# Turning the decayed keys of a gated-linear-attention loop by DMA instead of TensorE

## The chip, the cores and the metric

The kernel is one program on one core of one Trainium2 chip. The metric is the device time of one execution in microseconds (us): the median of several runs. The engines are named as the profile names them: PE is TensorE (matrix products), PEld its loading of the stationary operand, DVE is VectorE, ACT ScalarE, POOL GpSimd, and SP the sequencer that issues nearly all DMA transfers of this kernel. Each engine runs its own list of instructions strictly in the order fixed when the program was built; an instruction whose operand is not ready holds up all that stand behind it on its engine.

## The reference

One denoising step of a network of width 1024 with two layers, on 256 context tokens and 1024 latent tokens, 1280 tokens in all. Layer 0 mixes tokens by gated linear attention (GLA) in both directions, layer 1 by softmax attention. Each layer ends in a gate and an output projection. The part that the change touches is the recurrence of layer 0, of which there is one for each of 4 heads and 2 directions:

```python
def step(S, inp):
    qi, ki, vi, gi = inp
    b = jnp.cumsum(gi, axis=2)
    b_last = b[:, :, -1:, :]
    qe = qi * jnp.exp(b)
    ke = ki * jnp.exp(-b)
    a = jnp.where(mask, jnp.einsum("bhtk,bhsk->bhts", qe, ke), 0.0)
    o = jnp.einsum("bhts,bhsv->bhtv", a, vi) + jnp.einsum("bhtk,bhkv->bhtv", qe, S)
    S = jnp.exp(b_last[:, :, 0, :])[..., None] * S + jnp.einsum(
        "bhsk,bhsv->bhkv", ki * jnp.exp(b_last - b), vi)
    return S, o
```

Here `g` is the logarithm of a decay that depends on the token (`log_sigmoid(h @ wa1 @ wa2 + ba) / 16`), `ke` are the decayed keys, `a` is the masked score matrix of a chunk and `S` the state (128 keys by 256 values a head). The results are the two token streams, the GLA states after the context, and the attention layer's context keys and values, all in float32.

## The kernel before, in words

**Stages.** After a short prologue (modulation, normalised tokens turned into `hT_hi` and `hT_lo`, two f16 halves that together stand for float32), a long loop does the GLA layer, from about 80 to 520 us of the profile. The output projection, the attention layer and its projection follow. Products with weights are made as three f16 matmuls (high by high, high by low, low by high); their weights are scaled and split on the chip (`fill`, `fill_out`, `split_ahead`) from tiles `wst` and `wada` of 1 MB, which SP loads from HBM.

**The loop** (`gla`). Its 50 slots are 5 passes of 10 token tiles of 128 tokens. Passes 0 to 3 are the four heads, taken alternately forward and backward; in pass h the other direction of head h-1 is finished (`combine`, `gated`), so the fifth pass only finishes head 3. For a token tile of a head there are both directions in one tile (dimension `d`):

- `decay`, three slots ahead: a product `z`, three passes of ScalarE over it, two of VectorE, then the decay logarithms `g` split into two f16 parts, `ghi` on GpSimd (L725) and `glo` on VectorE (L726).
- `decayed`, one slot ahead: `cs`, the running sums, by matmul (L736); `en` = exp(-cs) and `ep` = exp(cs) on ScalarE (L738, L740); then on VectorE `en` times the keys (L742), from here on the decayed keys with the key dimension on the partitions, and `qe` = `ep` times the queries (L744).
- `intra`: TensorE turns both directions of `en` by a product with the identity `ident` (L759, two float32 matmuls into half of the PSUM bank `kt`), VectorE copies the result to SBUF as `ks` (L765), now with the tokens on the partitions. TensorE makes the scores from `en` and `qe` (L762, into the other half of the bank); VectorE masks them (L770, `am`) and GpSimd adds the two directions (L771, `at`).
- `outer`: `ks` by the values `v`, the tile's addition to the state of each direction (L783 and L787, PSUM bank `U`). ScalarE copies the other direction's part, `u`, away for the next pass (L790). `scan` brings the state up to date, `S` on GpSimd (L808, `Sa` and `Sc`), `W` on VectorE (L812).
- `local`: `at` by `v` and `qe` by the state (L829, bank `A`), copied out by ScalarE (`oa`, L832).

All else in the loop's TensorE work is projection: values and gates of the next slots, queries and keys of the next head (`mm`, L225), the modulation of the second layer (L403), and in the fifth pass the output projection's beginnings. ScalarE takes their results out of PSUM (L692 `v`, L696 `gx`, L651 `q` and `k`).

**What sets the order.** A scheduler places each instruction at build time by a priority, which is its place in the program text plus an offset. The offsets are the table `LATER`, by a name that a `with self.later(name)` puts around a piece of work. Tiles come from pools with a number of buffers (`bufs`); a new tile of the same tag waits until the tile that had its buffer is no longer read. `ew` is such a pool for short-lived tiles and `tl` for longer-lived ones. On SP the same list holds the weight loads (`wst` in L240, `wada` in L394), the stores of weights split ahead (`split`, L311), of the gated tokens (`og_d`, L860), and small transfers of state and modulation.

Of the kernel before, what the change touches and what calls it, by code (L numbers as in the profile page):

```python
# [6 lines left out]

F16 = mybir.dt.float16
BF16 = mybir.dt.bfloat16
F32 = mybir.dt.float32  # L10
I32 = mybir.dt.int32
# [6 lines left out]
P = 128  # L18
# [7 lines left out]
GH, DK, DV, RANK = 4, 128, 256, 16  # L26
# [25 lines left out]
    "loc": -30,  # L52
    "kt": 30,
    "A": -110,
    "intra": -5,
    "ks": -90,
    "combine": -15,
    "cs": -40,
    "vg": -10,
    "u": 75,  # L60
    "gated": 50,
    "decay": -25,
    "outer": 10,
    "Uc": -100,
    "a9.qr": 30,
    "a.s1": 30,
# [23 lines left out]
    "at": -115,  # L90
    "a0.rest": 30,
    "a0.gate": 5,
    "silu": -150,
    "a9.s0": -20,
    "x.setup": -150,
    "a9.val": 5,
    "combine9": 70,
    "jobs9": 220,
    "filler9": 15,
    "x.key8": 150,  # L100
    "eres": 110,
    "emod": -60,
    "wo2": 30,
    "fold": -30,
    "a0.q": 30,
    "wo3": 245,
    "x.key": -150,
# [2 lines left out]
    "s.r0": -150,  # L110
    "s.n2": -55,
    "s.r1": 115,
    "gated9": 60,
    "eprep": 400,
    "z.out": -5,
    "x.kset": -30,
# [3 lines left out]
    "s.s1": 220,  # L120
    "s.rk": 70,
    "s.n1": -100,
}

ADA = tuple((0, b) for b in (8, 9, 10, 11)) + tuple((1, b) for b in (4, 5, 6, 7, 0, 1, 2, 3, 8, 9, 10, 11))
# [13 lines left out]
class K:  # L139
# [36 lines left out]
    def pow2(self, mx, n=1, cross=True):  # L176
        nc, sp = self.nc, self.small
        if cross:
            ps = self.bank(self.p2_bank)
            up = mx.bitcast(BF16)  # L180
            one = self.ident.bitcast(BF16)[:, 1 : 2 * P : 2]
            for j in range(n):
# [48 lines left out]
    def wtile(self, place):  # L231
        a, b = place if isinstance(place, tuple) else (place, place)
        hi = self.t(self.wp, [P, KT, 512], F16, f"whi{a}")
        lo = self.t(self.wp, [P, KT, 512], F16, f"wlo{b}")
        return hi, lo, [None, None]
# [55 lines left out]
    def split_ahead(self, name, j, st):  # L291
# [3 lines left out]
        if j == 0:  # L295
            shape = [P, 2, 2, KT, 256] if name == "kv" else [P, 2, KT, 512]
            self.ahead[name] = self.t(self.dram, shape, F16, "w_" + name), [None, None]
        d, keep = self.ahead[name]
# [3 lines left out]
        for i in range(2):  # L302
            a = slice(i * h, i * h + h)
            t = self.t(self.spl, [P, 2, h, 256], F16, "split")
            for b in range(0, h, 2):
# [54 lines left out]
    def idle_steps(self, n, after):  # L360
        t = self.ident.bitcast(F16)
        with self.tc.issue_after(after):
            for _ in range(n):
                last = self.nc.tensor.matmul(self.spare[:, 0:256], t[:, 0:P], t, start=True, stop=True)
        return last.ins
# [181 lines left out]
    def gla_consts(self):  # L547
        nc, I = self.nc, self.I
        load = nc.sync.dma_start
        self.ia = self.io = 0  # L550
        self.r = self.t(self.gcp, [98, T], F16, "r")
        self.wa2 = self.t(self.gcp, [98, 2, GQ], F16, "wa2")
# [154 lines left out]
    def decay(self, h, i):  # L707
        nc = self.nc
        z = self.bank("z")[:, 0 : 2 * DK]
        with self.later("z"):  # L710
            nc.tensor.matmul(
                z.rearrange("p (d k) -> p d k", d=2), self.r[:, i * P : i * P + P],
                self.wa2[:, :, h * DK : h * DK + DK], start=True, stop=True,
            )
        u = self.t(self.ew, [P, 2 * DK], F32, "ls")
        nc.scalar.activation(u, z, AF.Abs, scale=self.inv_z)
        nc.scalar.activation(u, u, AF.Exp, scale=-1.0)
        nc.scalar.activation(u, u, AF.Ln, bias=1.0)
        g = self.t(self.ew, [P, 2 * DK], F32, "g")
        nc.vector.tensor_scalar(g, z, self.ninv_z, 0.0, ALU.mult, ALU.max)  # L720
        nc.vector.scalar_tensor_tensor(g, u, G_SCALE, g, ALU.mult, ALU.add)
        hi = self.t(self.tl, [P, 2, DK], F16, "ghi", bufs=4)
        lo = self.t(self.tl, [P, 2, DK], F16, "glo", bufs=4)
        hf, lf = (t.rearrange("p d k -> p (d k)") for t in (hi, lo))
        nc.gpsimd.tensor_scalar(hf, g, 1.0, 1.0, ALU.mult, ALU.mult)  # L725
        nc.vector.tensor_tensor(lf, g, hf, ALU.subtract)  # L726
        return hi, lo


    def decayed(self, h, i, g):  # L730
        nc = self.nc
        cs = self.bank("cs")[:, 0:260].rearrange("p (d k) -> p d k", d=2)
        with self.later("cs"):
            for d in range(2):
                for j in range(2):
                    nc.tensor.matmul(cs[:, d, :], g[j][:, d, :], self.cum[:, d, :], start=j == 0, stop=j == 1)  # L736
        en = self.t(self.ew, [P, 2, P], F32, "en")
        nc.scalar.activation(en, cs[:, :, 0:P], AF.Exp, scale=-1.0)  # L738
        ep = self.t(self.ew, [P, 2, 130], F32, "ep")
        nc.scalar.activation(ep, cs, AF.Exp)  # L740
        q, k = self.qkcol(h, 0, i), self.qkcol(h, 1, i)
        self.mark = nc.vector.tensor_tensor(en, en, k.unsqueeze(1).to_broadcast([P, 2, P]), ALU.mult).ins  # L742
        qe = self.t(self.tl, [P, 2, P], F32, "qe", bufs=NT + 1)
        nc.vector.tensor_tensor(qe, ep[:, :, 0:P], q.unsqueeze(1).to_broadcast([P, 2, P]), ALU.mult)  # L744
        eb = self.t(self.tl, [P, 2, 2], F32, "eb", bufs=NT + 2)
        nc.gpsimd.tensor_copy(eb, ep[:, :, P : P + 2])
        return {"qe": qe, "ke": en, "eb": eb}

    def intra(self, i, st):
        nc = self.nc  # L750
        ke, qe = st["ke"], st["qe"]
        kt, ap = (
            t.rearrange("p (d k) -> p d k", d=2)
            for b in (self.bank("kt"),)
            for t in (b[:, 0 : 2 * P], b[:, 2 * P :])
        )
        with self.later("kt"):
            for d in range(2):
                nc.tensor.transpose(kt[:, d, :], ke[:, d, :], self.ident)  # L759
        with self.later("A"):  # L760
            for d in range(2):
                nc.tensor.matmul(ap[:, d, :], ke[:, d, :], qe[:, d, :], start=True, stop=True)  # L762
        ks = self.t(self.ew, [P, 2, P], F32, "ks")
        with self.later("ks"):
            nc.vector.tensor_copy(ks, kt)  # L765
        am = self.am[self.ia % len(self.am)]
        self.ia += 1
        at = self.t(self.tl, [P, P], F32, "at", bufs=2)
        with self.later("at"):
            nc.vector.copy_predicated(am, self.mask, ap)  # L770
            nc.gpsimd.tensor_tensor(at, am[:, 0, :], am[:, 1, :], ALU.add)  # L771
        st["at"], st["ks"] = at, ks
# [1124 lines left out]
```

## Time and profile before

| what | value |
|---|---|
| median of 3 runs | 1249.68 us (1248.51 to 1250.69) |
| profiled execution, its own time | 1245.93 us |
| its span, first to last instruction | 1244.2 us |
| mean granted TensorE clock | 0.997 of full speed |
| PE busy | 1191.5 us, 96% of the span |
| DVE busy | 943.1 us, 76% |
| ACT busy | 687.3 us, 55% |
| POOL busy | 322.3 us, 26% |

How to read the views that follow. A group of instructions is one line: source line, engine, operation, output tile <- input tiles, shape (partitions x elements, type), count, then the busy time in us and the mean ns of one, then the idle time just before them with what ended most of it. A table of stretches gives for each engine its busy us in that stretch (PEld is the loading of weights, which runs beside PE), then the granted clock, the share of the DMA engines' time in use and GB/s. A chain of work is followed back from the last instruction of a stretch, at each step to what released it, and is printed in order of time as start, us, what. Waits read "engine line <- what it waited for: us in all, times, longest".

### The profile page before, as it was taken

The page shows a single profiled execution, that of the slowest core. Times are in us where ns is not written, and L with a number is a line of the kernel's source. Part 1 is how long each engine was busy: PE and PEld are TensorE (multiplying, and loading weights), DVE is VectorE, ACT ScalarE, POOL GpSimd, SP SyncE. Part 2 cuts the span into 40 slices and gives each one's busy share as a digit, 9 for nine tenths or more (in the row PEclk, how much of TensorE's full clock was granted, in tenths as well). Part 3 has the DMA queues.
Part 4 walks back from the last instruction along what each step waited for, and adds up shares of the span by engine and source line. Part 5 has one row for each costly group of instructions (what it writes and reads, how often), then busy time and mean ns, then how long its engine had stood idle before and what let it go on. Part 6 is the DMA issues. An engine that isn't in the chain of part 4 may idle for free.

```text
span 1244.2 us, 22355 instructions
## 1 busy us (share of the span) xinstructions
PE 1191.5 (96%) x7990; PEld 778.7 (63%) x7990; DVE 943.1 (76%) x2176; ACT 687.3 (55%) x1694; POOL 322.3 (26%) x566
## 2 busy tenths in 40 slices
PE   5899999999999999899999999999999999988998
PEld 3457765655556566677776666766766767665444
DVE  4787779887888789976876787877767687785653
ACT  2565566765666657832433567666676676663110
POOL 0132122323321143310213434331332352310000
PEclk9999999999999999999999999999999999999999
DMA  9512566456555544489977877768957666988432
GB/s 377 195 69 73 195 202 227 134 178 201 174 191 166 185 131 170 124 187 297 213 186 187 190 150 134 131 133 149 189 129 153 125 123 133 196 146 213 161 136 85
DMA packets 318064, 209.61 MB, mean 168 GB/s; under 512 B 257110, under 2 KB 294654, under 8 KB 309632
## 3 DMA queue, kind: packets, MB, share of 16 engines
q1 hardware_dynamic: 310800, 190.65, 59.9%
q10 hardware_dynamic: 4688, 10.57, 2.2%
q0 software_dynamic: 2464, 6.95, 1.9%
q8 instruction: 63, 1.03, 0.3%
q14 instruction: 49, 0.40, 0.1%
HBM read 107.83 MB, written 38.96 MB: 118 GB/s over the span
## 4 chain that ended last, share of the span: by engine, by line
PE 72%; DMA 9%; DVE 9%; ACT 4%; issue 2%; POOL 1%; SPq 0%; ACTq 0%; POOLq 0%; DVEq 0%
PE mm L225 38%; PE y L225 14%; PE S L1321 6%; DMA PT<-phl 6%; PE kv L225 3%; PE A L829 2%; PE mm L403 1%; PE kt L762 1%; PE U L783 1%; PE U L787 1%; DVE phl L1354 1%; DVE smx L1324 1%; PE o L843 1%; DMA out<-rope 1%; DMA wst<-og_d 1%
## 5 line engine op out<-in xcount | busy, mean ns | idle before, releaser
L225 PEld LDWEIGHTS <-hT_hi 128*128 128x128 f16 x1920 | 187.6, 98 | 120.8 <-issue 4.6
L225 PE MATMUL mm<-whi,hT_hi 128*128 128x512 f16 (+1 forms) x576 | 199.9, 347 | 2.4 <-ACT gx L696 2.0
L225 PE MATMUL mm<-whi,hT_lo 128*128 128x512 f16 (+1 forms) x576 | 200.1, 347 | 0.0
L225 PE MATMUL mm<-wlo,hT_hi 128*128 128x512 f16 (+1 forms) x560 | 194.0, 347 | 0.7 <-DVE wlo L287 0.7
L225 PEld LDWEIGHTS <-whi 128*128 128x128 f16 x1232 | 120.4, 98 | 62.8 <-issue 2.7
L1321 PE MATMUL S<-kT,wst 128*128 128x512 f16 (+1 forms) x624 | 140.4, 339 | 4.6 <-ACT p L1329 4.6
L225 PE MATMUL mm<-hT_hi,whi 128*128 128x256 f16 (+1 forms) x480 | 141.0, 294 | 2.2 <-ACT gx L1364 1.6
L1354 DVE SCALAR_TENSOR_TENSOR phl<-p,srec,phl 128x1280 f16<-128x1280 f32 (+1 forms) x80 | 107.0, 1337 | 46.9 <-ACT phl L1353 32.7
L225 PE MATMUL mm<-hT_hi,wlo 128*128 128x256 f16 (+1 forms) x480 | 141.0, 294 | 0.0
L225 PE MATMUL mm<-hT_lo,whi 128*128 128x256 f16 (+1 forms) x480 | 141.0, 294 | 0.0
L225 PEld LDWEIGHTS <-hT_lo 128*128 128x128 f16 x960 | 94.1, 98 | 61.9 <-issue 1.4
L225 PE MATMUL mm<-PT,vh 128*128 128x256 f16 x672 | 114.5, 275 | 11.3 <-DMA PT<-phl 8.1
L1324 DVE TENSOR_REDUCE smx<-S 128x1 f32<-128x1280 f32 (+1 forms) x80 | 101.3, 1271 | 27.0 <-PE S L1321 26.7
L1329 ACT ACTIVATE p<-S,snb,acol 128x1280 f32<-128x1280 f32 (+1 forms) x80 | 99.0, 1238 | 12.3 <-DVE phl L1354 6.7
L1321 PEld LDWEIGHTS <-wst 128*128 128x128 f16 x624 | 61.1, 98 | 54.8 <-issue 5.8
L225 PE MATMUL mm<-PT,vl 128*128 128x256 f16 x336 | 92.2, 274 | 0.0
L1351 POOL TENSOR_SCALAR phl<-p,srec 128x1280 f16<-128x1280 f32 (+1 forms) x40 | 54.0, 1350 | 106.8 <-DVE srec L1345 55.5
L225 PEld LDWEIGHTS <-vh 128*128 128x128 f16 x672 | 65.5, 99 | 22.4 <-issue 7.2
L225 PEld LDWEIGHTS <-wlo 128*128 128x128 f16 x616 | 60.2, 98 | 29.4
L1149 POOL TENSOR_TENSOR rope<-hx,ropet 128x64 f32<-128x64 f32 x160 | 51.5, 352 | 81.6 <-ACT hx L1285 64.3
L248 DVE TENSOR_REDUCE wmx<-wst 128x1 f32<-128x512 f32 x104 | 65.1, 676 | 3.9 <-DMA wst<-in_att_w 2.8
L216 POOL TENSOR_TENSOR hrs<-hrsa,mhalf 128x2 f32<-128x2 f32 x50 | 38.6, 773 | 107.0 <-DVE hrsa L214 106.7
(380 smaller groups left out, 2681.3 us busy)
## 6 DMA issues: line engine op xcount, KB each, us to landing
wada<-in_w_ada SPq DMA_DIRECT2D x16, 1024.0 KB, 5.3
wst<-in_att_w SPq DMA_DIRECT2D x14, 1024.0 KB, 5.5
wst<-in_gla_w_in SPq DMA_DIRECT2D x12, 1024.0 KB, 5.5
og_d<-og POOLq DMA_DIRECT2D x40, 128.0 KB, 2.9
wst<-og_d SPq DMA_DIRECT2D x5, 1024.0 KB, 6.7
og_d<-gx SPq DMA_DIRECT2D x37, 128.0 KB, 2.2
xr<-x_d SPq DMA_DIRECT2D x9, 512.0 KB, 3.4
out<-xr ACTq DMA_DIRECT2D x17, 256.0 KB, 2.0
```

The lines of the kernel that those rows point to most:

```text
L216: nc.gpsimd.tensor_tensor(r, a, self.mhalf[:, 0:w], ALU.pow)
L225: self.pe = self.nc.tensor.matmul(out, a, b, start=k == 0 and j == 0, stop=k == n - 1 and j == 2).ins
L248: nc.vector.tensor_reduce(mx[:, j : j + 1], st[:, 2 * j : 2 * j + 2, :], AX.XY, ALU.max, apply_absolute_value=True)
L403: nc.tensor.matmul(ps[32 * j : 32 * j + 32, 0:256], self.cst[:, k, :], to[:, k, :], start=k < 4, stop=k >= 4, tile_position=(0, 32 * j), s ...
L762: nc.tensor.matmul(ap[:, d, :], ke[:, d, :], qe[:, d, :], start=True, stop=True)
L829: nc.tensor.matmul(o, x, y, start=j == 0, stop=j == len(terms) - 1)
L1149: nc.gpsimd.tensor_tensor(tv[:, h, :, w, :], xv[:, h, :, 1 - w, :], sn[:, :, w, :], ALU.mult)
L1321: nc.tensor.matmul(S[:, a : a + n], x, y, start=m == 0, stop=m == 2)
L1324: last = nc.vector.tensor_reduce(mx, S, AX.X, ALU.max).ins
L1329: nc.scalar.activation(p, S, AF.Exp, scale=self.sexp, bias=nb, accum_out=den)
L1351: nc.gpsimd.tensor_scalar(hi, p, r, 2.0 ** 14, ALU.mult, ALU.mult)
L1354: nc.vector.scalar_tensor_tensor(lo, p, r2, hi, ALU.mult, ALU.subtract)
```

## The change

The decayed keys of a tile are no longer turned by TensorE. In `decayed`, ScalarE reads the float32 words of `en` as pairs of 16-bit numbers and writes all first halves and then all second halves into `kw` (128 partitions of 512 16-bit numbers); a DMA on SP turns the four 128x128 blocks of it into `kr`. In `intra`, GpSimd joins the halves again, writing each as every second 16-bit number of `ks`. The two TensorE transposes and VectorE's copy out of PSUM are gone. `kw`, `kr` and `ks` have one buffer each (`ks` had two); `ghi` and `glo` go from four buffers to three. Eleven offsets are set anew, and four are new. All instructions behind the table stand about 5 lines further down: the scores are L766, the mask and sum near L776, the outer products L788 and L792, `og_d` stores L865, weight loads L245 and L399.

By count, over the whole program: TensorE 80 transposes fewer, VectorE 40 copies fewer; ScalarE 40 copies more (L754), GpSimd 40 copies more (L770), SP 40 DMA transposes more (L757). All other work is the same in kind and number.

```diff
@@ LATER
-    "intra": -5,
-    "ks": -90,
+    "intra": -15,
+    "ks": 60,
...
+    "kr": -10,
+    "kw": -5,
@@ def decay
-        hi = self.t(self.tl, [P, 2, DK], F16, "ghi", bufs=4)
-        lo = self.t(self.tl, [P, 2, DK], F16, "glo", bufs=4)
+        hi = self.t(self.tl, [P, 2, DK], F16, "ghi", bufs=3)
+        lo = self.t(self.tl, [P, 2, DK], F16, "glo", bufs=3)
@@ def decayed
-        return {"qe": qe, "ke": en, "eb": eb}
+        kw = self.t(self.tl, [P, 2, 2 * P], U16, "kw", bufs=1)
+        with self.later("kw"):
+            nc.scalar.copy(kw, en.bitcast(U16).rearrange("p d (k w) -> p w d k", w=2).rearrange("p w d k -> p w (d k)"))
+        kr = self.t(self.tl, [P, 4, P], U16, "kr", bufs=1)
+        with self.later("kr"):
+            nc.sync.dma_start_transpose(kr, kw.rearrange("p w n -> p (w n)"))
+        return {"qe": qe, "ke": en, "eb": eb, "kr": kr}
@@ def intra
-        kt, ap = (
-            t.rearrange("p (d k) -> p d k", d=2)
-            for b in (self.bank("kt"),)
-            for t in (b[:, 0 : 2 * P], b[:, 2 * P :])
-        )
-        with self.later("kt"):
-            for d in range(2):
-                nc.tensor.transpose(kt[:, d, :], ke[:, d, :], self.ident)
+        ap = self.bank("kt")[:, 2 * P :].rearrange("p (d k) -> p d k", d=2)
...
-        ks = self.t(self.ew, [P, 2, P], F32, "ks")
+        ks = self.t(self.ew, [P, 2, P], F32, "ks", bufs=1)
         with self.later("ks"):
-            nc.vector.tensor_copy(ks, kt)
+            kb = ks.rearrange("p d k -> p (d k)").bitcast(U16).rearrange("p (n w) -> p w n", w=2)
+            nc.gpsimd.tensor_copy(kb, st["kr"].rearrange("p (w d) k -> p w (d k)", w=2))
```

The order on TensorE, in a slot of the second pass. Before, the two transposes (`kt<-ident,en`) stand between the outer product of the tile ahead and the scores of their own tile:

```order
1826 L736 LDWEIGHTS glo_2407
1827 L736 MATMUL cs_2700<-cum_145,glo_2407 128x130
1828 L783 MATMUL U_2677<-v_2435,ks_2528 128x256
1829 L759 MATMUL kt_2690<-ident_81,en_2538 128x128 x2
1830 L762 MATMUL kt_2690<-qe_2543,en_2538 128x128 x2
1831 L829 MATMUL A_2685<-v_2435,at_2530 128x256
```

After, a slot of the same pass:

```order
1933 L788 MATMUL U_2816<-v_2615,ks_2723 128x256
1934 L848 MATMUL o_2917<-Sc_2913,qe_1429 128x256
1935 L188 LDWEIGHTS wm_650_2673
1936 L188 MATMUL z_2675<-ident_81,wm_650_2673 128x128
1937 L792 MATMUL U_2816<-v_2615,ks_2723 128x256
1938 L834 MATMUL A_2825<-v_2615,at_2725 128x256
1939 L834 MATMUL A_2825<-Sa_2821,qe_2569 128x256
1940 L766 MATMUL kt_3049<-qe_2856,en_2851 128x128 x2
```

The scores stand alone, and `ks` is no product of TensorE any more: the outer product L788 waits for GpSimd.

The order on ScalarE in one of the first slots, from the exponentials of a tile on. Before:

```order
82 L738 ACTIVATE en_1154<-cs_1149 128x256
83 L740 ACTIVATE ep_1156<-cs_1149 128x260
84 L692 ACTIVATE v_1201<-mm_1176,inv_v_179_851 128x256
85 L790 COPY u_238_1128<-U_1125 128x256
86 L832 COPY oa_242_1137<-A_1134 128x256
87 L651 ACTIVATE k_259_1228<-mm_1203,iqk_95_453 128x256
88 L286 ACTIVATE whi_23_126<-wst_789,p2s_1084 128x2x256 x4
```

After:

```order
86 L743 ACTIVATE en_1160<-cs_1155 128x256
87 L745 ACTIVATE ep_1162<-cs_1155 128x260
88 L754 COPY kw_1169<-en_1160 128x512
89 L656 ACTIVATE k_267_1238<-mm_1213,iqk_95_453 128x256
90 L291 ACTIVATE whi_23_126<-wst_789,p2s_1092 128x2x256 x4
91 L795 COPY u_244_1136<-U_1133 128x256
92 L837 COPY oa_248_1145<-A_1142 128x256
```

The new copy stands right behind the exponentials and ahead of the evacuation of `k` and the weight split; the copies `u` and `oa` have moved behind these.

The order on SP at the end of the fourth pass and in the fifth, where the last weights come in. Before:

```order
167 L240 DMA wst_6006<-in_gla_w_in 128x2048
168 L860 DMA og_d_64<-gx_5821 128x256
169 L240 DMA wst_6260<-in_gla_w_out 128x2048
170 L860 DMA og_d_64<-gx_5955 128x256
171 L860 DMA og_d_64<-gx_6072 128x256
172 L435 DMA gt_d_67<-mod_1620_6229 128x2x8
173 L240 DMA wst_6475<-in_gla_w_out 128x2048
174 L1729 DMA whi_1745_6658<-in_x_sample 128x1024 x2
```

After:

```order
206 L245 DMA wst_6080<-in_gla_w_in 128x2048
207 L757 DMA_TRANSPOSE kr_6106<-kw_6104 128x4x128
208 L245 DMA wst_6338<-in_gla_w_out 128x2048
209 L865 DMA og_d_64<-gx_6029 128x256
210 L757 DMA_TRANSPOSE kr_6239<-kw_6237 128x4x128
211 L440 DMA gt_d_67<-mod_1696_6307 128x2x8
212 L865 DMA og_d_64<-gx_6148 128x256
213 L245 DMA wst_6557<-in_gla_w_out 128x2048
214 L1734 DMA whi_1825_6738<-in_x_sample 128x1024
215 L757 DMA_TRANSPOSE kr_6378<-kw_6376 128x4x128
```

Transposes now stand between the loads, each behind a 1 MB load or a store and ahead of the next load.

More of the change, by code (lines that the diff above doesn't have):

```diff
@@ L8 @@
 F16 = mybir.dt.float16
+U16 = mybir.dt.uint16
 BF16 = mybir.dt.bfloat16
@@ L59 @@
     "vg": -10,
-    "u": 75,
-    "gated": 50,
+    "u": -15,
+    "gated": 80,
     "decay": -25,
-    "outer": 10,
+    "outer": 5,
     "Uc": -100,
@@ L92 @@
     "a0.gate": 5,
-    "silu": -150,
+    "silu": -160,
     "a9.s0": -20,
@@ L96 @@
     "a9.val": 5,
-    "combine9": 70,
-    "jobs9": 220,
-    "filler9": 15,
+    "combine9": -150,
+    "jobs9": -50,
+    "filler9": 5,
     "x.key8": 150,
@@ L103 @@
     "wo2": 30,
-    "fold": -30,
+    "fold": 5,
     "a0.q": 30,
@@ L112 @@
     "s.r1": 115,
-    "gated9": 60,
+    "gated9": 55,
     "eprep": 400,
@@ L122 @@
     "s.n1": -100,
+    "Ua": -10,
+    "kr": -10,
+    "gate9": 20,
+    "kw": -5,
 }
```

## The prediction

> **What bounds the kernel now.** I read the table of stretches first, because the loop is one stage of several and only its own limit counts:
>
> ```profile
> 120.00:160.00 40.00, 40.00 (x300) 29.09 (x299) 31.17 (x84) 22.39 (x50) 7.95 (x16) 1.00 0.48 167
> 200.00:240.00 40.00, 40.00 (x261) 25.51 (x260) 37.45 (x104) 24.04 (x67) 14.88 (x26) 1.00 0.56 190
> 400.00:440.00 40.00, 40.00 (x233) 22.78 (x232) 30.34 (x84) 24.00 (x62) 9.60 (x18) 1.00 0.59 180
> 440.00:480.00 40.00, 39.94 (x211) 24.31 (x210) 36.42 (x112) 25.78 (x72) 16.82 (x28) 1.00 0.44 128
> 480.00:520.00 40.00, 35.25 (x254) 27.43 (x251) 38.34 (x115) 29.16 (x81) 13.21 (x21) 0.96 0.46 150
> 520.00:560.00 40.00, 38.04 (x270) 26.55 (x270) 30.69 (x80) 18.85 (x40) 8.14 (x13) 1.00 0.84 191
> ```
>
> In the eight stretches from 120 to 440 us PE (third figure) has no gap. From 480 us it has, 4.75 and 1.96 us, while DVE (fifth) is at 38.34 of 40. PE's waits from 80 to 520 us say the same; there are seven, these the longest and the shortest, 5.4 us in all:
>
> ```profile
> PE mm L225 <- ACT gx L696: 2.0, 1, 2.0
> PE cs L736 <- POOL ghi L725: 0.2, 1, 0.2
> ```
>
> A busy engine is not yet the one that sets the end, so third the chain of work that ended last, followed back from 580 us:
>
> ```profile
> 413.60 1.52 PE mm L225 x7
> 415.15 0.47 ACT v L692
> ...
> 443.10 5.20 DMA wst<-in_gla_w_out
> ...
> 452.31 0.34 DVE ks L765
> ...
> 455.64 5.73 DMA wst<-in_gla_w_in
> ...
> 468.00 0.34 DVE ks L765
> ...
> 554.65 17.55 PE y L225 x128
> ```
>
> Up to 415 us it is TensorE. From there to 554.65 us it runs through ScalarE, VectorE, GpSimd and weight loads, so that a product taken from TensorE there buys nothing at first.
>
> **What goes from TensorE.** Its instructions overlap, so the price is the distance of starts, not the 273 ns of one:
>
> ```profile
> L759 PE MATMUL kt<-ident,en x80: 270/273/330, 90.0 to 492.7; 128*128 128x128 f32 x80
> 187.98 0.38 PE L759 MATMUL kt<-ident,en 128*128 128x128 f32 x2
> 188.20 0.61 PE L762 MATMUL kt<-qe,en 128*128 128x128 f32 x4
> 188.65 0.38 PE L225 MATMUL mm<-whi,hT_hi 128*128 128x512 f16 x1
> 188.86 0.38 PE L225 MATMUL mm<-wlo,hT_hi 128*128 128x512 f16 x1
> ```
>
> A pair takes 188.20 - 187.98 = 0.22 us; 40 pairs 8.8 us. They lie evenly between 90.0 and 492.7 us, one in 10.3 us, so (415 - 90)/10.3 = 32 stand where TensorE sets the end: 32 x 0.22 = **-7.0 us**. The other 1.8 us I count at nothing.
>
> **What goes from VectorE.**
>
> ```profile
> L765 DVE COPY ks<-kt x40: 406/415/425, 91.4 to 496.8; 128x256 f32<-128x256 f32 x40
> ```
>
> 40 x 0.415 = 16.6 us less. To 415 us this hides behind TensorE. Behind it eight copies are left, 3.3 us, and the chain above passes through two of them, 0.34 us each: **-0.7 us**, at most -3.3.
>
> **What comes.** None of the three operations runs in this loop yet; the nearest rows are from other stages:
>
> ```profile
> L497 ACT CAST hl<-xr x16: 617/618/620, 583.1 to 683.9; 128x512 f16<-128x512 f32 x16
> L543 POOL TENSOR_SCALAR hT_hi<-h x8: 617/731/952, 40.2 to 68.0; 128x512 f16<-128x512 f32 x8
> L808 POOL TENSOR_SCALAR Sa<-Wa,eb,eb x32: 547/695/1417, 97.7 to 495.9; 128x256 f32<-128x256 f32 x32
> L1185 SPq DMA_TRANSPOSE wst<-xhl x40: 1188/1207/2158, 679.7 to 1073.4; - x40
> DMA to landing us min/median/max: 2.4/2.9/8.9
> L738 ACT ACTIVATE en<-cs 128x256 f32<-128x256 f32 x40 | 15.1, 378 | 2.7 <-PE cs L736 2.4
> L742 DVE TENSOR_TENSOR en<-en,k 128x256 f32<-128x256 f32 x40 | 17.7, 445 | 1.8 <-ACT en L738 1.7
> ```
>
> ScalarE's split: 40 x 0.618 = 25 us, on an engine busy 22 to 29 us of each 40. GpSimd's join: 0.731 us from the row of the same 512 elements, or up to 1.417 us from the same engine's worst case in this loop; 29 to 57 us over 400 us, on an engine busy at most 17 of 40. SP: 40 issues of 1.2 us, 48 us, on a queue that now mostly waits. In the stretches to 415 us all this is covered by TensorE's own work: 0. Cover is gone where a result comes late, so the length of the new chain matters. From `cs` to a joined `ks`: 0.38 + 0.45 + 0.62 + 2.9 + 0.73 = 5.1 us by these rows; I take 6, a fifth more for the handovers between five engines, and 12 if the transpose lands at its slowest, 8.9 instead of 2.9 us. Against it stands TensorE's work between `cs` and the outer product that reads `ks`: I counted the new order with the spacings above (0.21 us for a 128x512 f16 product, the others by their own). It is 8.3 to 31 us; 34 of 40 slots have over 12. The six short ones are slots 0, 1 and 36 to 39. Taken: 0; bound: if these six all meet the slowest landing, 10.3 us.
>
> The Trainium skill speaks against this step: VectorE: DVE Perf Modes, "Rules for kernel authors", says to turn 128x128 on TensorE where the result may go to PSUM, and to use the DMA crossbar otherwise. Its table of transpose paths has 1309 ns for one 128x128 bf16 block by DMA, an estimate of 5.2 us for the four blocks here where the trace has 2.9 us; by it the chain would be 8.3 us, still no longer than the shortest slot, and the sum would be the same.
>
> **What moves.** The last weight loads share SP with the transposes, and two of them are on the chain:
>
> ```profile
> wst<-in_gla_w_in SPq DMA_DIRECT2D x12, 1024.0 KB, 5.5
> SPq L240 <- DVE wlo L287: 42.0, 6, 21.2
> ```
>
> In the new order a transpose stands ahead of the second `in_gla_w_out` load and another ahead of the third. Ready in time, each delays its load by an issue, 1.2 us: **+2.4 us** together. Least is 0, since SP is often early and waits for the buffer anyway (second row: 42.0 us in six waits). Most is two landings at 8.9 us, because a transpose waits for the join of the one before: +17.8. I take the value nearest to the L1185 row. Slot 38's transpose stands behind a load into `whi` that waits for TensorE's last use of that tile; I count nothing for it, as its own slot's work follows that use.
>
> The new offsets put `u` and `oa` behind four weight splits on ScalarE in early slots, and `gated` and `jobs` of the fifth pass elsewhere. These can at best fill TensorE's gaps from 440 to 560 us, 0.06 + 4.75 + 1.96 = 6.8 us, and at worst open gaps of that kind. Taken: 0. Three buffers for `ghi` and `glo` instead of four: `decay` runs two slots ahead of its use, so a third is enough; 0.
>
> **Sum:** -7.0 - 0.7 + 2.4 = -5.3 us. The profiled execution took 1245.93 us, 3.75 below the median of the runs; against that median I forecast 1249.7 - 5.3 = **1244.4 us**. A measurement of this kernel can tell about 0.2% (2.5 us) from no change.
>
> **The rivals.**
>
> *All of it counts.* VectorE paces the end of the loop, and giving it 3.3 us there lets TensorE's 1.8 us through as well; the loads are hidden by their buffer waits. Then -7.0 - 3.3 = -10.3: 1239.4 us. For it: 38.34 of 40. Against: two 1 MB loads, 5.20 and 5.73 us, stand on the same chain, and a faster VectorE only waits for them.
>
> *Slower: the one-deep queue of transposes.* `kw`, `kr` and `ks` have one buffer each. So ScalarE's split of a tile waits until the transpose before has landed, SP's transpose until GpSimd has joined the one before, GpSimd's join until TensorE has done the outer product before. All three engines work in order: behind the split stand `v`, `k`, `u`, `oa` (TensorE's banks), behind the transpose the weight loads, behind the join `at`, `ghi` and the state `S`. The loop bears a transpose of 2.9 us: 0.62 + 2.9 = 3.5 us is under the smallest distance of two outer products in the new order, 3.9 us. With 8.9 us it is 9.5 us, and 26 of the 39 distances are shorter, by 46.9 us in all. 13 of 40 transposes stand directly behind a load of 0.5 or 1 MB on SP, which takes 5.5 us to land: 46.9 x 13/40 = 15 us of held engines. It decides as soon as a third of that reaches TensorE; with two thirds, 10 us, the time is 1249.7 - 5.3 + 10 = 1254.5 us. For it: the landing's own spread (2.4 to 8.9), a DMA share of about 0.5 in every stretch. Against: TensorE's long list between `cs` and its use.
>
> *The end of the loop gives it back.* The transposes ahead of the last weight loads wait for joins, and each load comes some 3.7 us later instead of 1.2: +7.4 in place of +2.4, and the time stays within 0.2%: 1249.4 us. For it: the chain from 443 to 461 us is two such loads. Against: the longest wait of SP for a weight buffer, 21.2 us, says that SP is not what the loads wait for everywhere.
>
> *GpSimd is a bad joiner.* Its join reads SBUF while VectorE multiplies; L808's 547 to 1417 ns show that GpSimd's time here doubles when it meets something. At 1.417 us for every join the chain grows by 0.7 us and eight joins of the end cost 5.6 us of GpSimd, which has 24 us free of each 40 there. Half of it on the chain would be +2.8: 1247.2 us, on the edge of no change. The Trainium skill's GPSIMD Engine Reference, "Engine selection", advises VectorE for elementwise work but calls GpSimd's one-input operations roughly line-rate, which agrees with 0.731 us for 512 elements.
>
> **How the numbers follow.** Forecast 0.44; all of it 0.08; slower by the one-deep queue 0.30; given back at the end 0.11; GpSimd 0.07, half of it within 0.2%. Faster: 0.44 + 0.08 + 0.03 = 0.55, same 0.11 + 0.04 = 0.15, slower 0.30. The range leaves out half of the second case below and a third of the slower one above: 1239 to 1258 us. The likeliest case alone spans 1241 to 1247, by its bounds of 0 and twice 2.4 us for the loads and -3.3 for VectorE.
>
> **What would show it.** Right: L759 and L765 gone; PE still at 40.00 of 40 from 120 to about 400 us, the fifth pass starting some 7 us earlier; L757 landing near 2.9 us; no wait of PE for POOL `ks` over a few us. Wrong: rows "PE U <- POOL ks", "ACT kw <- DMA kr" or "SP L757 <- POOL ks" of ten and more us; PE under 39 of 40 anywhere before 400 us; landings of L757 with a median above 5 us; the loads at L245 issued later relative to the loop's end than before. If PE has more gaps though `ks` is never late, the new offsets did it, and I had counted them at nothing.

## The result, and the profile after

The changed kernel takes 1254.31 us (median of nine runs, 1250.49 to 1256.78) against 1249.68 us of the kernel before (nine runs, 1248.51 to 1253.87). The ratio is 1.0035, with a 95% interval of 1.0018 to 1.0052: slower by 4.4 us by the ratio (the medians lie 4.6 us apart), where 5.3 us less had been forecast. The profiled execution took 1256.78 us, the longest of the nine, while that of before (1245.93 us) lies below its kernel's others; the two traces therefore show more difference (about 11 us) than the medians do, and sizes are taken from the ratios below, places and causes from the traces.

The table of stretches of the changed kernel, in the stretches shown of before (start:end, length, busy us and instructions of PE, PEld, DVE, ACT, POOL, granted clock, DMA share, GB/s):

```profile
120.00:160.00 40.00, 39.57 (x300) 28.88 (x298) 29.36 (x77) 23.26 (x54) 10.73 (x20) 1.00 0.56 183
200.00:240.00 40.00, 39.06 (x237) 23.30 (x236) 34.62 (x96) 24.13 (x67) 17.42 (x28) 1.00 0.65 193
280.00:320.00 40.00, 37.75 (x215) 20.04 (x212) 30.25 (x79) 25.01 (x67) 16.68 (x26) 1.00 0.74 191
400.00:440.00 40.00, 37.70 (x209) 19.75 (x208) 31.55 (x79) 27.59 (x72) 9.84 (x18) 1.00 0.64 194
440.00:480.00 40.00, 39.33 (x196) 22.53 (x195) 33.62 (x94) 24.32 (x70) 20.77 (x34) 1.00 0.51 142
480.00:520.00 40.00, 35.56 (x241) 26.32 (x239) 36.56 (x113) 29.81 (x79) 16.33 (x24) 0.96 0.44 133
520.00:560.00 40.00, 37.34 (x248) 25.93 (x247) 33.13 (x88) 20.54 (x48) 8.44 (x12) 0.91 0.80 177
```

TensorE, which had no gap from 120 to 440 us, now has one in most stretches there. From 80 to 440 us the two kernels stand like this, before first:

```profile
80.00:440.00 360.00, 359.92 (x2293) 223.78 (x2293) 295.96 (x788) 221.90 (x572) 98.08 (x182) 1.00 0.52 170
```

```profile
80.00:440.00 360.00, 352.49 (x2199) 213.42 (x2199) 287.16 (x747) 237.19 (x606) 123.69 (x211) 1.00 0.64 182
```

The gaps are 360 - 352.49 = 7.5 us in place of 0.1. In these two executions, as much as the saving that I had counted to this point (7.0 us) is lost before the end of the loop is reached.

Who is waited for: PE's longest waits from 80 to 520 us, and the new operations with what they wait for and who waits for them.

```profile
PE o L848 <- POOL Sc L811: 3.0, 2, 2.3
PE kt L766 <- DVE qe L749: 2.7, 2, 2.2
...
L757 SPq DMA_TRANSPOSE kr<-kw x40: 1189/1199/1969, 88.7 to 502.0; - x40
DMA to landing us min/median/max: 2.4/3.2/7.4
L754 ACT COPY kw<-en x40: 601/618/655, 88.0 to 499.8; 128x512 uint16<-128x512 uint16 x40
L770 POOL COPY ks<-kr x40: 757/764/1214, 91.3 to 506.3; 128x512 uint16<-128x512 uint16 x40
  DMA kr<-kw: 23.8, 10
  issue: 19.8, 6
...
  PE U L792: 0.6, 1
  PE U L788: 0.4, 1
```

The three new operations take about what their nearest rows said: 618 ns, 1199 ns of issue, a landing of 3.2 us, 764 ns. The outer products hardly wait for `ks` (0.6 and 0.4 us, their weight loads 0.8 and 0.7 us more). TensorE waits for other things instead: for the state `Sc` from GpSimd, for `qe` from VectorE. GpSimd stands 23.8 us before joins whose transpose has not landed, and 19.8 us more before six joins for which the profile names no releaser. ScalarE is held too: 9.0 us before five splits that wait for the transpose ahead of them to land. One of TensorE's gaps can be followed, on GpSimd's, SP's and TensorE's timelines around 439 us:

```profile
431.11 0.97 POOL L770 COPY ks<-kr 128x512 uint16<-128x512 uint16 x1
438.56 1.07 POOL L811 TENSOR_SCALAR Sc<-s,eb 128x256 f32<-128x256 f32 x1 [6.48 <-DMA s<-in_state_gla]
...
433.26 0.34 SPq L823 DMA_DIRECT2D out<-s  x1
433.76 1.20 SPq L757 DMA_TRANSPOSE kr<-kw  x1
436.33 3.66 SPq L810 DMA_DIRECT2D s<-in_state_gla  x2
...
439.69 0.48 PE L848 MATMUL o<-Sc,qe 128*128 128x256 f32 x1 [2.31 <-POOL Sc L811]
```

SP issues a store of the state, the transpose, then the load of the next state; GpSimd waits 6.48 us for that load, and TensorE 2.31 us for GpSimd. In the trace of before that load was waited for as well, but for half the time, and TensorE had no gap there:

```profile
430.50 0.34 SPq L818 DMA_DIRECT2D out<-s  x1
433.23 2.94 SPq L805 DMA_DIRECT2D s<-in_state_gla  x2
...
435.34 0.47 POOL L806 TENSOR_SCALAR Sc<-s,eb 128x256 f32<-128x256 f32 x1 [3.19 <-DMA s<-in_state_gla]
436.49 0.59 PE L843 MATMUL o<-Sc,qe 128*128 128x256 f32 x2
```

The transpose between store and load is not what makes the load late here: load follows store by 3.07 us with it and by 2.73 us without. The store itself already comes 2.8 us later. The chain that ended last in the trace of before ran through this store and this load, too.

### The profile page after: what moved, and what is told of

It reads as the page before. It is cut to its first block, busy times and chain, and to the rows that moved or that the text cites. A ratio compares the mean times of both kernels' runs of the same rounds, so it can differ in the third digit from the quotient of the medians.

```text
span 1254.3 us, 22371 instructions
## 1 busy us (share of the span) xinstructions
PE 1194.6 (95%) x7910; PEld 772.3 (62%) x7910; DVE 938.7 (75%) x2136; ACT 706.7 (56%) x1734; POOL 358.2 (29%) x606
```

## The experiments

### Taking the change apart with the scheduler free

Three runs let the scheduler make its own order. The first leaves the transposes and the copy out and adds nothing; its outer products read the unturned keys:

```diff
-        with self.later("kt"):
-            for d in range(2):
-                nc.tensor.transpose(kt[:, d, :], ke[:, d, :], self.ident)
...
-        ks = self.t(self.ew, [P, 2, P], F32, "ks")
-        with self.later("ks"):
-            nc.vector.tensor_copy(ks, kt)
+        ks = ke
```

> The kernel before without the two TensorE transposes and VectorE's copy; the outer products read the keys unturned, so that part of the computation is left out, and nothing is added. If the 8.8 us that TensorE is freed of are worth what I counted (7.0 where TensorE sets the end, 0.7 to 3.3 behind it), it takes 1239 to 1243 us. If TensorE's time is not what sets the end of the loop, it stays within 2.5 us of 1249.7.

The second is the kernel before with the new table `LATER`, the third the changed kernel with the old one; the edit is the table alone.

> The kernel before with the new table of offsets alone; all instructions as before. If the new order is what costs the time, it takes 1257 us or more (the loss of 4.6 us and the saving of 7 with it). If the order is neutral, as I had counted it, 1248 to 1252 us.

> The changed kernel with the old table of offsets (the new work without an offset of its own). If the new chain over ScalarE, SP and GpSimd is what costs, whatever the order, 1253 us or more. If the new offsets are what costs, 1245 us or less.

Measured: saving alone 1.0093 of before (1.0073 to 1.0112), new offsets alone 1.0160 (1.0141 to 1.0180), the change with old offsets 1.0057 (1.0039 to 1.0075). The first falls outside both of its expectations: less work, nothing added, and 12 us slower. What the second shows is not the price of any work, since it has the instructions of before, but that of the order: 1.6%. Every edit makes the scheduler place all else anew. The first run is less clean: in the order of before, such a run stands at 0.9930 (below), but its outer products read `qe` and not `en`, whose two buffers stay in use longer here (ScalarE waits 6.1 us in all for outer products to release one). So its 1.6% are order and that wait together. A change worth 0.7% cannot be judged that way.

### Holding the order

From here on the order is pinned. The order of each engine is read out of the built program and given back to the scheduler as edges that bind issue order only, not completion; instructions that an experiment adds are left out of the chain and are placed freely.

```diff
+    for k in idx:
+        i = kept[k]
+        e = str(i.engine)
+        if e in last:
+            tc.add_manual_dep(i, last[e].name, mb.DependencyInfo(mb.DependencyClass.NoSync, mb.DependencyReason.DATA), reason="order")
+        last[e] = i
```

Here `idx` is the recorded order and `kept` the program's instructions without the added ones. No run pins the kernel before to its own order, so that the edges by themselves cost nothing is taken and not measured.

Four corners: the order of before or of after, with the saving alone, and with the work of the other kernel in it. Where the turned keys are left out, the outer products read `qe` (`ks = qe`).

> Every engine's order of the kernel before is pinned by issue-order edges; the TensorE transposes and VectorE's copies are taken out of it and nothing is put in. The outer products read qe, a tile of the same size, so the turned keys are left out of the result. If TensorE sets the end up to 415 us as I read it, 1239 to 1243 us. If the saving is worth nothing even in an unchanged order, 1247 to 1252 us.

> The change in the pinned order of the kernel before: transposes and copies out, the ScalarE copy, the DMA transpose and the GpSimd join placed freely among it. If the added work is hidden and only the new order costs, 1239 to 1246 us. If the added chain costs in any order, 1251 us or more.

> The changed kernel's order pinned, with the three added operations taken out of it (the outer products read qe instead, so the turned keys are left out of the result). If the added work is what holds up the engines, 1240 to 1246 us. If the new order is what costs, it stays at 1252 to 1256 us.

> The changed kernel's order pinned, with its three added operations out and the TensorE transposes and VectorE's copies of before put back, placed freely. Against the run without either this gives the price of TensorE's transposes in that order: 7 to 9 us more if TensorE sets the pace there, under 3 if it does not. If the new order alone costs, 1258 us or more; if the added work alone did, 1247 to 1252 us.

The ratios to the kernel before, each with its interval:

| work in it | order of before | order of after |
|---|---|---|
| neither way of turning the keys | 0.9930 (0.9910 to 0.9950) | 0.9987 (0.9970 to 1.0004) |
| turned on TensorE | 1 (the kernel before) | 1.0042 (1.0027 to 1.0058) |
| turned by DMA (the change) | 1.0042 (1.0027 to 1.0057) | 1.0035 (1.0018 to 1.0052, the changed kernel) |

Read down the first column: without the transposes and the copies the kernel is 0.70% faster, 8.7 us. That is near the 8.8 us of TensorE's time, but the interval, 6.2 to 11.2 us, holds the 7.7 that I had counted as well. The added work then costs 1.0042 - 0.9930 = 0.0112, 14 us. Read across: the new order costs 0.57% by itself with neither way in it, 0.42% with the old work, and nothing with the change (-0.07%, within the intervals). Down the second column the added work costs 0.48%, 6 us. So the refitted order halves the price of the added work and gives that away in its own. By the second column the changed kernel is the saving, the order and the work: -8.7 + 7.1 + 6.0 = 4.4 us. The first two runs of that column came out between their two expectations, since order and work share the price; turning on TensorE costs 0.55% there, 6.9 us.

The two stretches of the loop and what follows, in the pinned order of before, with the saving alone and then with the whole change:

```profile
80.00:440.00 360.00, 357.85 (x2237) 219.24 (x2237) 288.91 (x765) 219.93 (x576) 101.60 (x185) 1.00 0.54 171
440.00:600.00 160.00, 154.44 (x1050) 109.30 (x1048) 134.23 (x356) 87.61 (x223) 42.62 (x71) 0.98 0.75 197
```

```profile
80.00:440.00 360.00, 352.46 (x2214) 215.76 (x2212) 289.34 (x750) 237.22 (x606) 126.65 (x214) 1.00 0.63 183
440.00:600.00 160.00, 145.94 (x968) 101.58 (x969) 126.26 (x337) 84.62 (x214) 46.53 (x72) 0.99 0.73 178
```

TensorE's gaps grow by 5.4 us to 440 us (357.85 against 352.46) and by 8.5 us between 440 and 600, in two executions whose spans lie 17.6 us apart. Stretches fixed in time don't hold the same work in both, so this says where gaps are and is no measure of the price. It does say that some lie before 440 us, where I had counted none.

Whom TensorE waits for tells more. From 80 to 530 us its waits for GpSimd come to 3.8 us with the saving alone and to 14.3 us with the whole change, these the longest:

```profile
PE o L848 <- POOL Sc L811: 4.5, 2, 2.8
PE U L788 <- POOL ks L770: 2.8, 1, 2.8
```

Its waits for everything else come to 3.5 and 3.9 us. What TensorE waits for more in this order is GpSimd, and mostly for the states and not for the keys.

### The added work, step by step

In the pinned order of before, ScalarE's split alone, then the DMA transpose with it, then the join that nobody reads (shortened; each added call is also noted down as one that the chain leaves out):

```diff
         with self.later("kw"):
             nc.scalar.copy(kw, en.bitcast(U16)...)
+        with self.later("kr"):
+            nc.sync.dma_start_transpose(kr, kw.rearrange("p w n -> p (w n)"))
...
+            nc.gpsimd.tensor_copy(kb, st["kr"].rearrange("p (w d) k -> p w (d k)", w=2))
-        st["at"], st["ks"] = at, ks
+        st["at"], st["ks"] = at, qe
```

> The pinned order of the kernel before, transposes and copies out (outer products read qe, so the turned keys are left out of the result), and of the added work ScalarE's split alone, read by nobody. The run with nothing added was 0.9930 of before, the whole change in this order 1.0042. If ScalarE's 25 us are what costs, 1.000 or more; if they are hidden, as I had counted, 0.992 to 0.995.

> The same with ScalarE's split and the DMA transpose, without the join; the transposed halves are read by nobody. If the transposes among SP's loads and stores are what costs, 1.000 or more; if they are hidden, no more than 0.002 above the run with the split alone.

> All three added operations with their waits for one another, but the outer products read qe: nobody waits for the joined keys, and the join waits for no outer product (the turned keys are left out of the result). If the lateness of the keys and the single ks buffer are what costs, 0.993 to 0.997; if it is GpSimd, held by joins ahead of the states, 1.001 to 1.005 as with the whole change.

| in the order of before | ratio | step |
|---|---|---|
| nothing added | 0.9930 (0.9910 to 0.9950) | |
| + ScalarE's split | 0.9931 (0.9910 to 0.9951) | +0.0001 |
| + DMA transpose on SP | 0.9953 (0.9937 to 0.9969) | +0.0022 |
| + GpSimd's join, read by nobody | 0.9994 (0.9981 to 1.0007) | +0.0041 |
| + outer products read the join (the change) | 1.0042 (1.0027 to 1.0057) | +0.0048 |

25 us of ScalarE's time cost nothing that can be told within these intervals, 2.5 us either way. The transposes come to about 2.7 us, with intervals that overlap. The join costs 5 us though nobody waits for it, between the two expectations for that run, and reading it 6 us. GpSimd's longest waits from 80 to 530 us in the run with the unread join say where the 5 us come from:

```profile
POOL ks L770 <- DMA kr<-kw: 80.4, 36, 5.0
POOL eb L751 <- ACT ep L745: 34.4, 17, 5.7
POOL ghi L730 <- DVE g L726: 32.0, 16, 3.7
```

36 of 40 joins hold GpSimd until their transpose has landed, 80.4 us in all; behind each stand `at`, `ghi` and the states. A join whose operand is ready sooner tells this from the join's own time:

```diff
-            nc.gpsimd.tensor_copy(kb, st["kr"].rearrange("p (w d) k -> p w (d k)", w=2))
+            nc.gpsimd.tensor_copy(kb, qe.bitcast(U16)...)
```

> As the run with all three operations and nobody waiting for the keys, but the join reads words of qe, which are ready a good deal earlier than the transpose lands; its work and its shape stay, its wait for the transpose goes, and the transposed halves are read by nobody (the turned keys are left out of the result). Split and transpose alone gave 0.9953, the join behind the landing 0.9994. If GpSimd's held queue (80.4 us of waits for landings) is the price, 0.995 to 0.997; if GpSimd's time of 0.8 us a join, or its meeting with VectorE, is the price, 0.998 to 1.000.

0.9946 (0.9924 to 0.9967), against 0.9953 without a join and 0.9994 with one that waits. Its row:

```profile
L770 POOL COPY ks<-qe x40: 750/760/1288, 88.2 to 493.2; 128x512 uint16<-128x512 uint16 x40
  DVE qe L749: 44.5, 26
```

Forty joins of 760 ns, 30 us of GpSimd, cost nothing that shows; the same joins behind a landing cost 5 us. The queue held in order is the price, and it is how late the join lets go that counts: in this run GpSimd is held as well, 44.5 us for `qe`, and that is free. The joins could also have acted backwards, through the single `kr` on SP and through `kw` on ScalarE. The traces speak against it: SP waits 74.4 us before its transposes in the run with the waiting joins and 97.8 us in this one, and ScalarE's split waits for a landing in neither. How the 5 us reach TensorE shows too: VectorE waits 15.9 us for `ghi` behind the held joins, 10.3 us in this run and 8.2 us without a join, and TensorE in turn 5.3 us for VectorE, against 1.2 and 1.0. The Trainium skill's GPSIMD Engine Reference, "Engine selection", steers elementwise work from GpSimd to VectorE for its speed; that is not what decides here, as this run shows.

In the whole change the joins are held otherwise. With a reader, the single `ks` also binds the join to the outer product before; GpSimd's waits before its joins in that run are, the longest first:

```profile
  DMA kr<-kw: 20.4, 11
  PE U L792: 16.7, 7
  issue: 15.5, 7
```

With the smaller ones that is 59.5 us, of which the landing is a third. So the 5 us of the table are the price of waiting for landings in a run without a reader; they can't be carried over as a part of the 14 us.

### Where the join runs

> The whole change in the pinned order of the kernel before, with the join on VectorE in place of GpSimd (0.41 us there by the copy it replaces). If GpSimd held by its joins is what costs, 0.994 to 0.999; if it is the chain's length and the single buffers, or the work on ScalarE and SP, 1.002 to 1.008.

> The whole change in the pinned order of the kernel before with the join on ScalarE. With the join on VectorE it was 0.9975. If any engine other than GpSimd does, 0.996 to 0.999; if an engine with TensorE's evacuations behind the join pays for waiting on landings as GpSimd does, 1.001 or more.

> The changed kernel's own order pinned, with the join on VectorE, placed freely, in place of GpSimd's. The changed kernel is 1.0035, its order with nothing added 0.9987. If the join on GpSimd is most of the added cost in this order too, 0.999 to 1.002; if the order's own cost and the transposes are, 1.003 or more.

The edit is the engine's name in the join (`nc.vector.tensor_copy`, `nc.scalar.copy`), with the join's place left free. In the order of before, the join on VectorE gives 0.9975 (0.9957 to 0.9992), on ScalarE 0.9985 (0.9970 to 1.0001), on GpSimd 1.0042. What the two joins wait for, on VectorE and then on ScalarE:

```profile
L770 DVE COPY ks<-kr x40: 442/452/622, 90.9 to 503.1; 128x512 uint16<-128x512 uint16 x40
  DMA kr<-kw: 5.3, 5
  PE U L792: 1.1, 1
```

```profile
L770 ACT COPY ks<-kr x40: 753/770/822, 89.8 to 499.6; 128x512 uint16<-128x512 uint16 x40
  DMA kr<-kw: 5.7, 7
  PE U L792: 1.0, 1
```

On both engines the transpose has mostly landed when the join's turn comes: 7.0 and 6.7 us of waits before the joins, where GpSimd had 59.5. TensorE's waits for GpSimd fall with it, from 14.3 to 6.5 and 7.8 us. That these engines come late because they have more work of their own ahead of the join fits their busy shares, but was not tested by itself. The version with VectorE's join is 0.25% faster than the kernel before and 0.60% faster than the changed one; it puts 18 us back on VectorE (40 x 0.452).

In the order of after the same edit gives 1.0069 (1.0048 to 1.0090), no better than the changed kernel's 1.0035; by what I expected, it is then the order's own cost and the transposes (1.003 or more), and not the join on GpSimd. There the join's place on VectorE was free among an order made for a GpSimd join, so this run does not say what VectorE's join would give in an order of its own. What makes up the 6 us in the changed kernel's own order was not taken apart, and that GpSimd's held queue is the cause is shown for the order of before alone.

### Reading the join: one buffer, or late keys

A version with two buffers each of `kw`, `kr` and `ks` gave no time, since it needs more SBUF than is left beside the kernel's other tiles. Two buffers of `ks` alone need 1 KB a partition that is not there; `at` gives up one buffer and `glo` one. The second run gives up the same and keeps one `ks`.

```diff
-        ks = self.t(self.ew, [P, 2, P], F32, "ks", bufs=1)
+        ks = self.t(self.ew, [P, 2, P], F32, "ks", bufs=2)
-        at = self.t(self.tl, [P, P], F32, "at", bufs=2)
+        at = self.t(self.tl, [P, P], F32, "at", bufs=1)
-        lo = self.t(self.tl, [P, 2, DK], F16, "glo", bufs=3)
+        lo = self.t(self.tl, [P, 2, DK], F16, "glo", bufs=2)
```

> The whole change in the pinned order of the kernel before with two buffers of ks, for whose space at goes to one buffer and glo to two. If the last step of 0.005 (outer products reading the joined keys) is the single ks buffer, through which GpSimd waits for TensorE, 0.999 to 1.001 and 0.003 or more below the run with one ks buffer and the same at and glo; if it is the lateness of the keys themselves, no difference between the two.

> The run beside it: one buffer of ks, with at at one buffer and glo at two as there. If giving up these buffers costs nothing, 1.003 to 1.006 like the whole change in this order; if it costs, above that.

Two buffers 1.0051 (1.0034 to 1.0069), one 1.0027 (1.0011 to 1.0043). The second buffer does not help; if anything it costs, which neither expectation had. GpSimd's waits before the joins tell why, with one buffer and then with two:

```profile
  DMA kr<-kw: 18.0, 10
  PE U L792: 16.3, 6
  issue: 15.8, 7
```

```profile
  DMA kr<-kw: 79.6, 33
  PE U L792: 6.1, 2
```

With two buffers the joins stand earlier in GpSimd's order (the median join starts 3.5 us after its transpose's issue in place of 6.0), and it waits 79.6 us for landings in place of 18.0: what it no longer waits for TensorE, it waits for the DMA, and more.

The other suspects are the last slots, where the way from `cs` to the outer product is shortest:

> The whole change in the pinned order of the kernel before (1.0042), but in the last four slots, where the order leaves the shortest way between cs and the outer product, the outer products read qe (the turned keys of these four tiles are left out of the result). If the step from 0.9994 to 1.0042 is these late keys, 0.999 to 1.001; if it is spread over the loop, 1.003 or more.

> The pinned order of the kernel before; the join on VectorE, and the last four tiles turned on TensorE and copied by VectorE as before. With all 40 by DMA and VectorE's join it was 0.9975. If the short last slots cost there too, 0.993 to 0.996; if not, 0.997 to 0.999.

With the last four outer products reading `qe`, 1.0019 (1.0002 to 1.0036), halfway between 0.9994 and 1.0042: about half of the step lies in these four tiles, though the intervals allow from none to all of it. In the whole change TensorE's one long wait for `ks`, the 2.8 us shown above, falls there, and it is gone in this run.

Turning these four tiles on TensorE again, with VectorE's join elsewhere (and the offset `kt` of these transposes at -60 in place of 30), gave 0.9993 (0.9975 to 1.0011), no better than 0.9975 with all 40 by DMA: with the join on VectorE the short slots are not what is left.

The other half of the step stays open. One thing goes with it: the granted TensorE clock, averaged over each version's twelve executions, is 0.9958 with the unread join, 0.9934 with four tiles reading `qe` and 0.9923 with the whole change. 0.0035 of 1250 us is up to 4.4 us. But among the twelve executions of the whole change the time does not follow the clock (1251.41 us at 0.990, 1255.35 us at 0.997), so this remains a suspicion.

## Why the prediction was wrong

- **TensorE's saving.** I took 0.22 us a pair and 32 of 40 pairs, -7.0 us, and -0.7 for VectorE's copies. Measured in an unchanged order it is 8.7 us (6.2 to 11.2) for both together. The mechanism was right; whether the last 1.8 us counted too, as the rival "all of it counts" had it, lies within the interval.
- **The failing step** is "In the stretches to 415 us all this is covered by TensorE's own work: 0". I had compared the length of the new chain with TensorE's work between `cs` and the outer product, and rightly so for the reader of `ks`: outer products waited about 1 us for it in the changed kernel. But what waits is not only the reader. My sign for it came: TensorE was at 37.75 of 40 from 280 to 320 us. The added work costs 14 us in the order of before and 6 us in the changed kernel's own. In the order of before most of it comes through GpSimd, which is held before its joins: TensorE waits 14.3 us for it in place of 3.8, most of that for the states; joins that nobody reads cost 5 us already; and with the join on VectorE 8 of the 14 us are gone. In the changed kernel's own order the cause of the 6 us stays open.
- **The new offsets**, "Taken: 0", are the second failing step. In the new order the kernel is 0.57% slower with neither way of turning in it. I had bounded this by gaps of 6.8 us to win or lose, and 7.1 us were lost. My own sign for it, more gaps though `ks` is never late, did come, but it does not tell the offsets from the added work: both open gaps without a late `ks`.
- **The transposes on SP** I put at +2.4 us, for two loads at the end; 2.7 us were measured over the whole loop, with overlapping intervals, and whether they come by those two loads was not looked at. The landing I had at 2.9 with up to 8.9; it was 3.2, up to 7.4.
- **The slower rival** has the right sign, and its picture of engines held in order is what the runs show. That its 1254.5 us is the measured time is in part luck: it adds 10 us of held engines to my -5.3, where the runs have -8.7, 6.0 for the work, and 7.1 for an order that it counted at nothing. Its cause was the single buffers; of these a second `ks` did not help, and a second `kw` or `kr` has no measurement. It gave ScalarE's split and SP's queue as much blame as GpSimd's; in the order of before the split cost nothing that shows, while in the changed kernel's order ScalarE was held 9.0 us.
- **GpSimd as a bad joiner** I priced by the join's own duration, 1.417 us at worst. Its duration (764 ns) costs nothing that shows; its place in a queue does.
- **The rule that spoke against the change.** The Trainium skill, VectorE: DVE Perf Modes, "Rules for kernel authors", would keep such a transpose on TensorE. The estimate of 5.2 us that I made from its figure for one block was too high (3.2 us for four blocks in one instruction). Its advice came out right for the change as made: TensorE's way costs 8.7 us here and the DMA's way 14. With VectorE's join the DMA's way is the cheaper one: 0.9975 - 0.9930 = 0.45%, 5.6 us.

## What to carry to other kernels

Before a step is moved to an idle engine, ask what that engine runs next: GpSimd, with little to do, reached the moved step early, waited there and held all that stands behind it, while two busier engines reached it when the data was there (in one of the two orders tried; in the other VectorE's join was no better). Judge a change that a scheduler reorders with the order pinned, in both orders and with neither way in it; otherwise the order's own 0.5 to 1.6% is taken for the change. Price a new asynchronous chain by every queue that it waits in, and not by its last reader alone.

## What the runs showed of the hardware that was not expected

The granted TensorE clock fell where the new gaps are. From 500 to 540 us, before and after:

```profile
500.00:540.00 40.00, 36.91 (x256) 26.68 (x255) 36.61 (x100) 28.13 (x72) 12.29 (x18) 0.96 0.63 158
```

```profile
500.00:540.00 40.00, 33.98 (x209) 23.80 (x207) 34.97 (x107) 27.25 (x71) 16.35 (x21) 0.87 0.63 154
```

0.96 against 0.87 over 40 us is up to 3.6 us of clock in these two executions, beside the 3 us more of gaps in the same stretch. The Trainium skill, TensorE: Matmul & The Clock Gate, Part 1, has the clock halved after an idle window; the rows agree in that the clock is lower where the gaps are larger. As a cause of the 4.4 us it is small all the same: averaged over whole executions the clock is 0.9940 in 114 of the kernel before and 0.9933 in nine of the changed one, which is at most 0.9 us.
